# Token-major output projections: 512 columns at a time, the first half row by row of the weights for four blocks in four PSUM banks, the second half block by block

## The chip, the core and the metric

The kernel runs on one core of a Trainium2 chip. The metric is the device time of one execution in microseconds, 1507.78 us as the median of three runs (1503.12 to 1508.62). The work of the core is spread over TensorE (PE, with the weight loads shown apart as PEld), VectorE (DVE), ScalarE (ACT), GpSimd (POOL) and the queue on SyncE (SP) that issues nearly all DMAs. Every engine takes its instructions strictly in the order in which they stand; between engines they wait for each other by semaphores.

## The reference

Two token sequences (1024 and 512 tokens of width 1024, float32) go through two layers and a last RMSNorm. Cut to what matters here:

```
def attn_retention_layer(x, ...):           # layer 0: attention and retention
    z = rmsnorm(x, g) @ w_in ...
    mixed = concat([silu(ga) * oa, silu(gb) * ob], axis=-1)
    return x + mixed @ w_out                # first output projection
def windowed_layer(x, ...):                 # layer 1: windowed attention
    z = rmsnorm(x, g) @ w_in ...
    return x + (silu(gate) * o) @ w_out     # second output projection
y = rmsnorm(windowed_layer(attn_retention_layer(x)), final_norm)
```

`mixed` and `w_out` are both 1024 wide, so each output projection is a 1024 by 1024 matrix product for 1536 tokens.

## The kernel before

The 1536 tokens are 12 blocks of 128, in three groups `t` of four blocks (`GB`), which are handled in the order 2, 0, 1. A float32 product is made of three matmuls: both operands are split in a high part and the low remainder (`split`, L109; `load_w`, L130), and high by high, high by low and low by high are added in PSUM (`proj_tm_k`, L150). The gated branch of a group lies as `X["h", k, t]` and `X["l", k, t]`, eight rows `k` of 128 features by 512 tokens.

The output projections of groups 2 and 0 are feature-major (`out_proj_fm`, L266): their matmuls stream 512 tokens, and they are issued as filler between the pieces of the attention pipeline. At their end they need a sum over features: GpSimd adds squares into `acc` (L288), four small matmuls make `ssq`, then VectorE (`ms`), GpSimd (`rstd`) and VectorE (`dg`) make the factor, and four matmuls spread it as `R` (L293 to L299). For group 0 all this happens at the end of the pipeline.

The output projection of group 1 (`out_proj`, L324) is the one that changes. It is token-major: a block's 128 tokens are the stationary operand, the weights stream. It stands twice in the program, once for layer 0 (`woab`, the "first projection", some 793 to 850 us) and once for layer 1 (`woc`, the "second projection", some 1447 us to the end). Weights come in four chunks of 256 columns, each as four tiles of two rows `k`: a DMA into `wraw`, a copy to the high part on GpSimd (L139) and a subtraction for the low part on VectorE (L140). Tiles go alternately to the buffers `w` and `wg`, four each; `wg` is also the staging room of the feature-major projection. For each chunk the four blocks are taken one after the other; a block's 24 matmuls fill one of the three PSUM banks of `ps_any`, and VectorE adds the bank to the residual `xr` (L350). After the chunks comes `finish`: after layer 0 `norm_ab` (norm, scaling, transposes `trx`, and then the projection `pskv` of layer 1), after layer 1 `fin_c` (norm and output, L1092).

PSUM has eight banks here: five under the tag `s` (`ps_s` and `ps_t`, L57 to L61: scores, transposes `pte`, `ssq`, `R`) and three under `pj`. Tiles of a tag are handed out in the order of the program. A scheduler orders the instructions of each engine from priorities and from its own estimate of times; `tc.high_priority()` lifts a piece of code ahead.

Of the kernel before, what the change touches and what calls it, by code (L numbers as in the profile page):

```python
# [8 lines left out]
F32 = mybir.dt.float32  # L9
F32R = mybir.dt.float32r  # L10
AF = mybir.ActivationFunctionType
ALU = mybir.AluOpType
# [4 lines left out]
P = 128  # L17
# [5 lines left out]
GB = 4  # L23
CW = 256
# [12 lines left out]
def trunk_kernel(ctx, tc, x, xT, wab, woab, wc, woc, gT, qkg, ret, sink, relb, fng,  # L37
                 ropeA, ropeB, dist, kdist, qdist, onehot, wmask, out_p0, out_p1, out_s):
    nc = tc.nc
    dma = nc.sync.dma_start  # L40
# [3 lines left out]
    wp = ctx.enter_context(tc.tile_pool(name="wp", bufs=1))  # L44
# [8 lines left out]
    def buf(tag, name, n=None, dt=F32):  # L53
        t = wk.tile([P, SIZE[tag]], dt, tag=tag, name=name, bufs=BUFS[tag])
        return t if n is None else t[:, :n]

    def ps_s(name):  # L57
        return pp.tile([P, 512], F32, tag="s", name=name, bufs=5)
# [6 lines left out]
    def ps_p(name, use="fill"):  # L65
        free = ring[use]
        ring["i"] = next(i % 3 for i in range(ring["i"] + 1, ring["i"] + 4) if i % 3 in free)
        return pp.tile([P, 512], F32, tag=f"pj{ring['i']}", name=name, bufs=1)

    def ps_any(name):  # L70
        return ps_p(name, "all")
# [16 lines left out]
    def mm(ps, lhsT, rhs, start, stop):  # L88
        i = nc.tensor.matmul(ps, lhsT=lhsT, rhs=rhs, start=start, stop=stop)  # L89
        if pace["after"] is not None:  # L90
            tc.add_manual_dep(i.ins, pace["after"], order, reason="a filler keeps to its place in the pipeline")
            pace["after"] = None
        return i
# [36 lines left out]
    def load_w(arr, c, tag, lo=None, hook=None, ks=range(KT), raws=None):  # L130
        ts = {}
        for i in (k // 2 for k in ks[::2]):
            if raws is None:
                raw = wp.tile([P, 2 * CW], F32, tag="wraw", name="wraw", bufs=2)
                dma(out=raw, in_=arr[c, :, 2 * i:2 * i + 2, :].rearrange("p k n -> p (k n)"))
            else:
                raw = raws[i]
            w = wp.tile([P, 2, 2 * CW], F32R, tag=tag, name=tag, bufs=4)
            nc.gpsimd.tensor_scalar(w[:, 0, :], raw, 1.0, 1.0, ALU.mult, ALU.mult)  # L139
            (lo or nc.gpsimd).tensor_tensor(w[:, 1, :], raw, w[:, 0, :].bitcast(F32), ALU.subtract)  # L140
            ts[i] = w
            if hook is not None:
                hook(i)

        def get(s, k, a=0, n=CW):
            o = (k % 2) * CW + a
            return ts[k // 2][:, s, o:o + n]
        return get

    def proj_tm_k(ps, w, b, k, ks=range(KT)):  # L150
        t, o = b // GB, (b % GB) * P
        xh, xl = X["h", k, t][:, o:o + P], X["l", k, t][:, o:o + P]
        mm(ps, xh, w(0, k), k == ks[0], False)
        mm(ps, xh, w(1, k), False, False)
        mm(ps, xl, w(0, k), False, k == ks[-1])

    def proj_tm(ps, w, b, ks=range(KT)):
        for k in ks:
            proj_tm_k(ps, w, b, k, ks)

    def proj_pair(w, b, name):
        ps = ps_any(name)
        for j in range(2):
            proj_tm(ps[:, j * CW:(j + 1) * CW], w, b + j)
        return ps
# [28 lines left out]
    def load_block(src, name, tag="E"):  # L194
        hs = []
        for i in range(2):
            h = buf(tag, f"{name}{i}")
            dma(out=h, in_=src[:, i * 512:(i + 1) * 512])
            hs.append(h)
        return hs  # L200
# [121 lines left out]
                pass  # L322

    def out_proj(t, warr, ks, res, finish):  # L324
        def fetch(c):
            raws = {}
            for i in (k // 2 for k in ks[::2]):
                raws[i] = buf("E", "wraw")
                dma(out=raws[i], in_=warr[c, :, 2 * i:2 * i + 2, :].rearrange("p k n -> p (k n)"))
            return raws  # L330

        def convert(c, raws):
            return load_w(warr, c, "wg" if c % 2 else "w", nc.vector, None, ks, raws)

        with tc.high_priority():
            ws = [convert(0, None)]
        x1 = [load_block(res(t * GB + j), "xr") for j in range(GB)]
        raws = fetch(1)
        for c in range(4):
            w = ws[c]  # L340
            if c < 3:
                with tc.high_priority():
                    ws.append(convert(c + 1, raws))
                    raws = fetch(c + 2) if c < 2 else None
            for j in range(GB):
                ps = ps_any("pso")[:, :CW]
                proj_tm(ps, w, t * GB + j, ks)
                sl = x1[j][c // 2][:, (c % 2) * CW:(c % 2 + 1) * CW]
                with tc.high_priority():
                    nc.vector.tensor_tensor(sl, ps, sl, ALU.add)  # L350
        finish(t, x1)
# [43 lines left out]
    raws, xts = [], []  # L395
# [54 lines left out]
    for t in range(NG):  # L450
        pss = [(ps_any if t == 1 and j < 3 else ps_s)("pskv")[:, :CW] for j in range(GB)]
# [11 lines left out]
    ws = [load_w(wab, 0, "w")]  # L463
# [199 lines left out]
    for h in range(4):  # L663
        w = ws[h]
# [241 lines left out]

    x1_ab = []
    out_proj(1, woab, KS_A, lambda b: x[b], norm_ab)


    wkv = load_w(wc, 0, "w")
    kd_raw = {}
    for p in PAIRS:
        if p == PAIRS[4]:
            to_x(x1_ab, 1, 1)
        ps = proj_pair(wkv, 2 * p, "pskv").rearrange("p (b c) -> p b c", b=2)
# [175 lines left out]
    def fin_c(t, x2):  # L1092
        for j, hs in enumerate(x2):
# [4 lines left out]
            for i, h in enumerate(hs):  # L1098
                dma(out=out_p1[j][:, i * 512:(i + 1) * 512], in_=h)

    out_proj(1, woc, KS_C, lambda b: x1_d[b], fin_c)


# [90 lines left out]
```

## Time and profile before

| | us |
|---|---|
| median of three runs | 1507.78 |
| lowest and highest | 1503.12, 1508.62 |
| the profiled execution, its own time | 1507.83 |
| its span in the profile | 1506.1 |
| first projection, from the end of the work before it on TensorE to the first `pskv` | 793.1 to 850.4 |
| second projection, from the end of the feature-major matmuls to its last matmul | 1447.6 to 1496.4 |
| from that last matmul to the end of the span | 9.7 |

The span is what the engines' records cover; the execution's own time is 1.7 us longer. A row of the timeline gives the start, the duration from first to last of the merged instructions, the engine and line, the operation and, in brackets, how long the engine had been idle and who ended that. Matmuls overlap, so their pace is read from start to start.

### The profile page before, as it was taken

What the parts mean: (1) busy time and instruction counts of PE and PEld (TensorE: products, weight loads), DVE (VectorE), ACT (ScalarE), POOL (GpSimd) and SP (SyncE); (2) the same over time, 40 slices, a digit from 0 to 9 for tenths busy, and PEclk for the clock granted to TensorE, in tenths of its full rate; (3) what the DMA queues carried; (4) which work ended last, traced back from release to release, by engine and by line L of the source; (5) the groups of instructions that cost most, each with busy time, mean ns of one, the idle gap of its engine ahead of it and who ended that gap; (6) DMA issues with size and microseconds to landing.
All of it is one profiled execution on the core that took longest, in us unless ns stands there. A gap on an engine that the chain in (4) does not pass through costs nothing.

```text
span 1506.1 us, 26020 instructions
## 1 busy us (share of the span) xinstructions
PE 1451.7 (96%) x8734; PEld 1269.8 (84%) x8734; DVE 1052.6 (70%) x2431; ACT 719.5 (48%) x1770; POOL 812.3 (54%) x1044
## 2 busy tenths in 40 slices
PE   8999999989999999999999999999999999999997
PEld 8989999977888888777778998888888888777777
DVE  7455867686676666887978237687777767888774
ACT  5632222354555555555653245566556556645202
POOL 7654654474645484887887423342522532566542
PEclk9999999999999999999999999999999999999999
DMA  9631212326212143643664231121212211568752
GB/s 329 207 119 51 75 54 69 99 74 191 74 45 72 53 113 116 206 141 107 192 213 141 86 109 46 61 71 50 74 45 94 63 54 53 173 206 280 229 157 99
DMA packets 137333, 176.59 MB, mean 117 GB/s; under 512 B 38064, under 2 KB 66736, under 8 KB 137200
## 3 DMA queue, kind: packets, MB, share of 16 engines
q1 hardware_dynamic: 135040, 169.41, 35.8%
q0 software_dynamic: 2016, 5.51, 1.3%
q8 instruction: 69, 1.13, 0.3%
q14 instruction: 64, 0.52, 0.1%
q10 hardware_dynamic: 144, 0.01, 0.0%
HBM read 125.83 MB, written 53.25 MB: 119 GB/s over the span
## 4 chain that ended last, share of the span: by engine, by line
PE 71%; DVE 11%; DMA 4%; POOL 4%; issue 3%; ACT 1%; SPq 0%; POOLq 0%; DVEq 0%; ACTq 0%
PE psg L89 17%; PE psq L89 10%; PE po L89 8%; PE psb L89 8%; PE pso L89 8%; PE pte L173 7%; PE s L89 4%; PE sc L89 4%; PE pskv L89 2%; DVE xl L118 2%; DVE w L140 1%; DVE el L112 1%; DMA wraw<-in_woc 1%; DVE nm L837 1%; PE ptq L173 1%
## 5 line engine op out<-in xcount | busy, mean ns | idle before, releaser
L89 PE MATMUL psg<-xh,wg 128*128 128x512 f32 x768 | 263.9, 400 | 0.2 <-POOL wg L140 0.2
L107 POOL TENSOR_SCALAR ec<-ec,rl 128x384 f32<-128x384 f32 (+1 forms) x192 | 108.8, 581 | 241.5 <-DVE rl L1056 87.7
L112 DVE TENSOR_TENSOR el<-pte,eh 128x512 fp32r<-128x512 f32 x288 | 196.6, 685 | 56.2 <-ACT eh L111 32.5
L111 ACT ACTIVATE eh<-pte 128x512 fp32r<-128x512 f32 x288 | 170.1, 596 | 119.7 <-PE po L89 65.0
L89 PE MATMUL pso<-xh,w 128*128 128x512 f32 x512 | 183.6, 418 | 10.4 <-DVE w L140 4.6
L89 PEld LDWEIGHTS psg<-xh,wg 128*128 128x128 f32 x768 | 143.9, 189 | 29.2 <-POOL e L107 0.9
L107 POOL TENSOR_SCALAR e<-e,rl 128x512 f32<-128x512 f32 x160 | 114.3, 726 | 93.3 <-DVE rl L848 33.9
L89 PE MATMUL psg<-xl,wg 128*128 128x512 f32 x384 | 150.9, 393 | 0.0
L1051 ACT ACTIVATE ec<-ec,nm 128x384 f32<-128x384 f32 (+1 forms) x192 | 109.6, 572 | 82.7 <-DVE nm L1049 77.7
L845 ACT ACTIVATE e<-s,nm 128x512 f32<-128x512 f32 x160 | 108.9, 687 | 68.0 <-DVE nm L842 50.0
L837 DVE TENSOR_REDUCE nm<-s 128x1 f32<-128x512 f32 x160 | 107.8, 683 | 37.4 <-PE s L89 36.9
L139 POOL TENSOR_SCALAR w<-wraw 128x512 fp32r<-128x512 f32 x116 | 79.4, 686 | 97.6 <-PE pskv L89 32.4
L89 PE MATMUL psq<-xh,w 128*128 128x512 f32 x384 | 130.0, 397 | 0.0
L89 PEld LDWEIGHTS pso<-xh,w 128*128 128x128 f32 x512 | 99.4, 197 | 35.8 <-DVE w L140 7.8
L1045 DVE CUSTOM_DVE_ANT_0 ec<-sc,bias,sink_s 128x384 f32<-128x384 f32 (+1 forms) x192 | 105.3, 568 | 22.2 <-PE sc L89 17.8
L89 PE MATMUL pso<-xl,w 128*128 128x512 f32 x256 | 104.1, 408 | 2.0 <-DVE xl L118 2.0
L173 PE MATMUL pte<-ident,e 128*128 128x128 f32 x640 | 96.0, 275 | 1.6 <-POOL e L107 0.8
L173 PEld LDWEIGHTS pte<-ident,e 128*128 128x128 f32 x640 | 78.8, 142 | 20.3 <-ACT e L845 2.2
L140 POOL TENSOR_TENSOR w<-wraw,w 128x512 fp32r<-128x512 f32 x68 | 91.2, 1344 | 1.9
L89 PEld LDWEIGHTS psg<-xl,wg 128*128 128x128 f32 x384 | 72.5, 189 | 13.1
L89 PEld LDWEIGHTS psq<-xh,w 128*128 128x128 f32 x384 | 71.9, 188 | 13.6
L173 PE MATMUL pte<-ident,ec 128*128 128x128 f32 x512 | 79.0, 272 | 0.2
(230 smaller groups left out, 3942.6 us busy)
## 6 DMA issues: line engine op xcount, KB each, us to landing
wraw<-in_woab SPq DMA_DIRECT2D x48, 256.0 KB, 3.4
wraw<-in_woc SPq DMA_DIRECT2D x48, 256.0 KB, 3.8
wraw<-in_wab SPq DMA_DIRECT2D x44, 256.0 KB, 3.3
wraw<-in_wc SPq DMA_DIRECT2D x36, 256.0 KB, 3.1
xt<-in_xT SPq DMA_DIRECT2D x24, 256.0 KB, 5.4
xb<-in_x SPq DMA_DIRECT2D x24, 256.0 KB, 4.8
qd<-qd SPq DMA_DIRECT2D x48, 128.0 KB, 2.9
gab<-gz SPq DMA_DIRECT2D x24, 256.0 KB, 2.0
```

The costliest lines, as they stand in the source:

```text
L89: i = nc.tensor.matmul(ps, lhsT=lhsT, rhs=rhs, start=start, stop=stop)
L107: nc.gpsimd.tensor_scalar(o, i, s, 1.0, ALU.mult, ALU.mult)
L111: nc.scalar.activation(hi, src, AF.Copy)
L112: nc.vector.tensor_tensor(lo, src, hi.bitcast(F32), ALU.subtract)
L118: nc.vector.scalar_tensor_tensor(lo, src, scale, hi.bitcast(F32), ALU.mult, ALU.subtract)
L139: nc.gpsimd.tensor_scalar(w[:, 0, :], raw, 1.0, 1.0, ALU.mult, ALU.mult)
L140: (lo or nc.gpsimd).tensor_tensor(w[:, 1, :], raw, w[:, 0, :].bitcast(F32), ALU.subtract)
L173: return nc.tensor.transpose(o, i, ident)
L837: nc.vector.tensor_reduce(nm2[:, c:c + 1] if nh == 2 else nm[:, h:h + 1], s, AX.X, ALU.max, negate=True)
L845: nc.scalar.activation(eh[c], ss[c], AF.Exp, bias=nm[:, h:h + 1], accum_out=l[:, h, c:c + 1])
L1045: nc.vector.tensor_tensor_reduce(es[h][:, :nk], s, bias[h][:, bo:bo + nk], 1.0, sink_s[:, 4 * c + h:4 * c + h + 1], ALU.add, ALU.max, mx[: ...
L1051: nc.scalar.activation(es[a][:, :nk], es[a][:, :nk], AF.Exp, bias=nm[:, a:a + 1], accum_out=l[:, a:a + 1])
```

## The change

`out_proj` is rewritten. A weight tile is now one row `k` and 512 columns: two chunks of the same layout in the DRAM, so that a DMA's pieces are 256 columns long (1 KB) where they were 512 numbers (2 KB). Conversion is by the same two instructions. All eight tiles of the first 512 columns are fetched and converted with high priority; raw tiles use the two `wraw` buffers and buffers of the tag `E` in turn. The first half is done row by row: for each `k` the 12 matmuls of all four blocks, into four PSUM tiles of the tag `s`, and behind each row the tile of the same row of the second half is fetched. Then VectorE adds four banks of 512 columns. The second half is done block by block in banks of `ps_any`, the last block in two pieces of 256 columns. Numbers per projection: 384 matmuls of 256 columns before; now 168 of 512 columns and 48 of 256; 16 tiles as before, and 9 additions for 16.

```diff
     def out_proj(t, warr, ks, res, finish):
...
+        n = len(ks)
+
+        def fetch(i):
+            c, k = i // n, ks[i % n]
+            raw = wp.tile([P, 2 * CW], F32, tag="wraw", name="wraw", bufs=2) if i % 3 == 0 or i < 2 else buf("E", "wraw")
+            dma(out=raw.rearrange("p (c n) -> p c n", c=2), in_=warr[2 * c:2 * c + 2, :, k, :].rearrange("c p n -> p c n"))
+            w = wp.tile([P, 2, 2 * CW], F32R, tag="w" if i % n < 4 else "wg", name="wo", bufs=4)
+            nc.gpsimd.tensor_scalar(w[:, 0, :], raw, 1.0, 1.0, ALU.mult, ALU.mult)
+            nc.vector.tensor_tensor(w[:, 1, :], raw, w[:, 0, :].bitcast(F32), ALU.subtract)
+            ws[c, k] = w
+
+        ws = {}
         with tc.high_priority():
-            ws = [convert(0, None)]
+            for i in range(n):
+                fetch(i)
         x1 = [load_block(res(t * GB + j), "xr") for j in range(GB)]
-        raws = fetch(1)
-        for c in range(4):
-            w = ws[c]
-            if c < 3:
-                with tc.high_priority():
-                    ws.append(convert(c + 1, raws))
-                    raws = fetch(c + 2) if c < 2 else None
+        pss = [ps_s("pso") for j in range(GB)]
+        for i, k in enumerate(ks):
             for j in range(GB):
-                ps = ps_any("pso")[:, :CW]
-                proj_tm(ps, w, t * GB + j, ks)
-                sl = x1[j][c // 2][:, (c % 2) * CW:(c % 2 + 1) * CW]
+                proj_tm_k(pss[j], lambda s_, k_: ws[0, k_][:, s_, :], t * GB + j, k, ks)
+            with tc.high_priority():
+                fetch(n + i)
+        for j in range(GB):
+            with tc.high_priority():
+                nc.vector.tensor_tensor(x1[j][0], pss[j], x1[j][0], ALU.add)
+        for j in range(GB):
+            for a, m in ((0, 512),) if j < GB - 1 else ((0, CW), (CW, CW)):
+                ps = ps_any("pso")[:, :m]
+                proj_tm(ps, lambda s_, k_: ws[1, k_][:, s_, a:a + m], t * GB + j, ks)
+                sl = x1[j][1][:, a:a + m]
                 with tc.high_priority():
                     nc.vector.tensor_tensor(sl, ps, sl, ALU.add)
         finish(t, x1)
```

Where this moves instructions is seen in the order of the engines. First projection, TensorE, before: behind the transposes (`pte`) of the last attention unit some of its products (`po`) stand, and at once the new projection's matmuls (`pso<-w,xh`), with more `po` strewn among them further on.

```order
L173 MATMUL pte<-ident,e 128x128 x4
L89 MATMUL po<-eh,av 128x512
L89 MATMUL po<-el,av 128x512
L89 MATMUL po<-eh,av 128x512
L89 MATMUL po<-el,av 128x512
L89 MATMUL pso<-w,xh_9056 128x256 x2
L89 MATMUL pso<-w,xl_9057 128x256
L89 MATMUL pso<-w,xh_9198 128x256 x2
```

Now, the same place on TensorE from `ssq` on:

```order
L89 MATMUL ssq<-dg,acc 128x1 x4
L89 MATMUL po<-el,av 128x512
L89 MATMUL po<-eh,av 128x512
L89 MATMUL po<-el,av 128x512
L89 MATMUL po<-eh,av 128x512
L89 MATMUL po<-el,av 128x512
L89 MATMUL po<-eh,av 128x512
L89 MATMUL po<-el,av 128x512
L89 MATMUL R<-dg 128x128
L89 MATMUL pso<-wo,xh_9056 128x512 x2
L89 MATMUL pso<-wo,xl_9057 128x512
```

No matmul of the projection stands ahead of the last `po` and of the first `R` any more.

Second projection, TensorE, before, around `ssq`: the projection's matmuls stand on both sides of it, 56 of them between the last feature-major matmul and `ssq`.

```order
L89 MATMUL pso<-w,xl_16808 128x256
L89 MATMUL pso<-w,xh_16924 128x256 x2
L89 MATMUL pso<-w,xl_16925 128x256
L89 MATMUL pso<-w,xh_17018 128x256 x2
L89 MATMUL ssq<-dg,acc 128x1 x4
L89 MATMUL pso<-w,xl_17019 128x256
L89 MATMUL pso<-w,xh_17104 128x256 x2
```

Now, TensorE at the end of the feature-major matmuls (`pso<-xh,w`):

```order
L89 MATMUL pso<-xh_16521,w 128x512
L89 MATMUL pso<-xl_16522,w 128x512
L89 MATMUL pso<-xh_16521,w 128x512
L89 MATMUL ssq<-dg,acc 128x1 x4
L89 MATMUL R<-dg 128x128
L89 MATMUL pso<-wo,xh_16625 128x512 x2
L89 MATMUL pso<-wo,xl_16626 128x512
```

`ssq` and the first `R` follow the feature-major matmuls directly, and the projection starts behind them. On GpSimd the same place now reads as follows (`wo` are the new tiles' copies, `acc` the sums that `ssq` needs):

```order
L332 TENSOR_SCALAR wo<-wraw 128x512 x2
L288 TENSOR_TENSOR acc<-acc,sq 128x512
L332 TENSOR_SCALAR wo<-wraw 128x512 x2
L291 MEMSET dg 128x128
L332 TENSOR_SCALAR wo<-wraw 128x512
L288 TENSOR_TENSOR acc<-acc,sq 128x512
L332 TENSOR_SCALAR wo<-wraw 128x512 x2
L103 TENSOR_TENSOR rstd<-ms,nhalf 128x4
```

and on VectorE, where `ms` is the read of `ssq`:

```order
L283 TENSOR_TENSOR y<-pso,y 128x512
L333 TENSOR_TENSOR wo<-wraw,wo 128x512 x4
L100 TENSOR_SCALAR ms<-ssq 128x4
L333 TENSOR_TENSOR wo<-wraw,wo 128x512
L298 TENSOR_SCALAR dg<-ident,rstd 128x128 x4
```

Seven of the eight copies stand ahead of `rstd`, and four subtractions between the last `y` and `ms`.

End of the second projection, VectorE, before: the last bank's addition (L350) stands behind the output scaling (L1096) of the block before.

```order
L350 TENSOR_TENSOR xr_17598<-pso,xr_17598 128x256
L184 TENSOR_REDUCE ssum<-ss 128x1
L100 TENSOR_SCALAR ms<-ssum 128x1
L1096 SCALAR_TENSOR_TENSOR xr_17598<-xr_17598,rstd,fn 128x512
L350 TENSOR_TENSOR xr_17602<-pso,xr_17602 128x256
```

Now:

```order
L356 TENSOR_TENSOR xr_17436<-pso,xr_17436 128x512
L184 TENSOR_REDUCE ssum<-ss 128x1
L100 TENSOR_SCALAR ms<-ssum 128x1
L356 TENSOR_TENSOR xr_17440<-pso,xr_17440 128x256
L1102 SCALAR_TENSOR_TENSOR xr_17436<-xr_17436,rstd,fn 128x512
L356 TENSOR_TENSOR xr_17440<-pso,xr_17440 128x256
```

Two additions of the last block now follow the third block's, with the scaling between them; between the third block's last matmul and the last block's there are 48 matmuls where there were 24.

## Rows read from the trace of the kernel before

**Rows 1.** The page: shares of the span in the chain that ended last.

```profile
PE 71%; DVE 11%; DMA 4%; POOL 4%; issue 3%; ACT 1%; SPq 0%; POOLq 0%; DVEq 0%; ACTq 0%
```

**Rows 2.** Windows: stretch, length, busy per engine (instructions), PE clock, DMA share, GB/s.

```profile
793.10:850.40 57.30, 53.82 (x423) 51.63 (x422) 36.26 (x60) 17.68 (x42) 39.33 (x40) 1.00 0.44 137
1447.60:1496.40 48.80, 48.42 (x401) 47.90 (x399) 29.93 (x50) 7.45 (x23) 18.96 (x22) 1.00 0.36 115
```

**Rows 3.** Timeline of PE, second projection: start, duration, operation, [idle before <-releaser].

```profile
1445.30 0.62 PE L89 MATMUL pso<-xh,w 128*128 128x512 f32 x2
...
1447.36 0.39 PE L89 MATMUL pso<-xh,w 128*128 128x512 f32 x1
...
1454.84 1.05 PE L89 MATMUL ssq<-dg,acc 128*128 128x1 f32 x8 [0.38 <-POOL acc L288]
...
1459.92 1.06 PE L89 MATMUL R<-dg 128*128 128x128 f32 x8
...
1477.22 0.40 PE L89 MATMUL pso<-w,xh 128*128 128x256 f32 x2
...
1482.62 0.40 PE L89 MATMUL pso<-w,xh 128*128 128x256 f32 x2
...
1496.17 0.28 PE L89 MATMUL pso<-wg,xl 128*128 128x256 f32 x1
```

**Rows 4.** Timeline of PE, first projection.

```profile
805.58 1.17 PE L89 MATMUL R<-dg 128*128 128x128 f32 x8
...
820.19 0.50 PE L89 MATMUL pso<-wg,xh 128*128 128x256 f32 x2 [1.93 <-DVE xr L350]
```

**Rows 5.** Timeline of POOL, first projection, ahead of `R`.

```profile
802.88 0.62 POOL L139 TENSOR_SCALAR wg<-wraw 128x512 fp32r<-128x512 f32 x1 [5.49 <-DMA wraw<-in_woab]
```

**Rows 6.** Timelines of DVE, ACT and POOL, second projection, the steps ahead of `R`.

```profile
1445.74 1.77 DVE L140 TENSOR_TENSOR w<-wraw,w 128x512 fp32r<-128x512 f32 x1 [1.04 <-POOL w L139]
...
1449.25 0.68 DVE L140 TENSOR_TENSOR w<-wraw,w 128x512 fp32r<-128x512 f32 x1
1449.85 0.68 DVE L283 TENSOR_TENSOR y<-pso,y 128x512 f32<-128x512 f32 x1
...
1457.12 0.15 DVE L100 TENSOR_SCALAR ms<-ssq 128x4 f32<-128x4 f32 x1
1458.43 1.23 DVE L298 TENSOR_SCALAR dg<-ident,rstd 128x128 f32<-128x128 f32 x4 [1.15 <-POOL rstd L103]
...
1450.57 0.64 ACT L286 ACTIVATE sq<-y 128x512 f32<-128x512 f32 x1 [5.13 <-DVE y L283]
...
1445.67 1.29 POOL L288 TENSOR_TENSOR acc<-acc,sq 128x512 f32<-128x512 f32 x1
...
1453.07 1.72 POOL L288 TENSOR_TENSOR acc<-acc,sq 128x512 f32<-128x512 f32 x1
...
1457.36 1.03 POOL L103 TENSOR_TENSOR rstd<-ms,nhalf 128x4 f32<-128x4 f32 x1 [1.55 <-DVE ms L100]
```

**Rows 7.** Timeline of DVE, the end of the kernel.

```profile
1497.47 1.74 DVE L1096 SCALAR_TENSOR_TENSOR xr<-xr,rstd,fn 128x512 f32<-128x512 f32 x1 [0.67 <-POOL rstd L103]
1499.13 0.41 DVE L350 TENSOR_TENSOR xr<-pso,xr 128x256 f32<-128x256 f32 x1
...
1501.19 0.75 DVE L1096 SCALAR_TENSOR_TENSOR xr<-xr,rstd,fn 128x512 f32<-128x512 f32 x1 [0.67 <-POOL rstd L103]
```

**Rows 8.** Windows, a stretch of idle TensorE and the stretch behind it.

```profile
1437.90:1441.30 3.40, 1.64 (x6) 1.07 (x7) 2.26 (x2) 0.00 (x0) 2.83 (x3) 1.00 0.42 147
1441.30:1444.70 3.40, 3.40 (x10) 2.62 (x9) 3.40 (x4) 0.00 (x0) 1.67 (x2) 0.50 0.58 189
```

**Rows 9.** Timeline of POOL, the weights of `pskv` behind the first projection.

```profile
838.28 2.54 POOL L140 TENSOR_TENSOR w<-wraw,w 128x512 fp32r<-128x512 f32 x2
```

**Rows 10.** DMA issues by tile: count, KB each, median us to landing.

```profile
wraw<-in_woab SPq DMA_DIRECT2D x48, 256.0 KB, 3.4
zq<-qd SPq DMA_DIRECT2D x12, 128.0 KB, 2.5
```

More of the change, by code (lines that the diff above doesn't have):

```diff
@@ L324, in out_proj @@
     def out_proj(t, warr, ks, res, finish):
[L325 to L333, printed above, removed]
+        n = len(ks)
[7 more added lines that the diff above has]
+            ws[c, k] = w
```

## The prediction

> **What bounds the kernel now.** I read the chain of waits by engine first: TensorE carries 71% of it, VectorE 11%, GpSimd and DMA 4% each [rows 1]. So the two stretches that change are read from TensorE's side. The windows over them show it busy for 53.8 of 57.3 us in the first projection and for 48.4 of 48.8 in the second, at full granted clock, with the DMA engines under half busy [rows 2]. The reader is to see there that the second stretch has almost no hole to fill: a gain must come from shorter matmul time, and any new wait shows in full.
>
> Then the pace, from start to start in the timeline of TensorE. From 1477.22 to 1482.62 there are 45 matmuls of 256 columns in 5.40 us, 0.120 each; from 1445.30 to 1447.36 there are 9 of 512 columns in 2.06 us, 0.229 each [rows 3]. Two narrow ones take 0.240.
>
> Last, what ran while something else was slow. In both places the factor `R` of the feature-major projection has a long chain behind it. In the second, the feature-major matmuls end at about 1447.6 (1447.36 and one pace), `ssq` starts at 1454.84 and `R` at 1459.92 [rows 3], and the windows say that TensorE was busy nearly throughout: the narrow projection's matmuls filled these 12.3 us (56 of them, 6.7 us, stand ahead of `ssq`). In the first, `R` starts at 805.58 [rows 4], 12.5 us after the stretch begins at 793.1, with GpSimd idle 5.49 us before it, waiting for a raw weight tile [rows 5].
>
> **The change, part by part.**
>
> *Wider matmuls.* Before, 384 × 0.120 = 46.1 us per projection. After, 168 × 0.229 + 48 × 0.120 = 38.5 + 5.8 = 44.2; with the pace rounded up to 0.23, 44.4, which I use. It saves 1.7 per projection, all on the path.
>
> The timeline shows 0.229 for a wide matmul, at full clock [rows 3]. The Trainium skill, "TensorE: Matmul & The Clock Gate", section "Back-to-back issue gap", gives about 131 ns for 512 columns as the sustained figure of a stream of weight loads and matmuls. By it each projection would be some 168 × 0.098 = 16 us shorter, an estimate; the trace measures the very same shape in such a stream and disagrees, so I give it a chance of 0.01 and leave it out of the sum.
>
> *The order on TensorE.* The four PSUM tiles of the first half come from the tag that also serves scores, `ssq` and `R`, and are handed out behind them. By the order, no projection matmul stands ahead of the first `R` any more. What covered the chain to `R` is gone; the chain is now paid as idle time. This is the largest term, twice.
>
> First projection. Before, `R` came 12.5 us after 793.1; without GpSimd's wait for the raw tile it would be 7.0. The high-priority fetch may remove that wait, or not, since seven copies now stand before `rstd`. I take the middle, 9.7 (7.0 to 12.5). Within it lies the rest of attention's products.
>
> Second projection. After the last feature-major matmul come: `y` 0.68, `sq` 0.64, `acc` 1.29 to 1.72, `ssq` 1.05, `ms` 0.15, `rstd` 1.03, and the first of four `dg`, a quarter of 1.23, 0.31 [rows 3, 6]: 5.2 at the least. Four weight subtractions are queued on VectorE between `y` and `ms`. One took 0.68 alone and 1.77 beside GpSimd's `acc` [rows 6]: 2.7 to 7.1 together, beside `sq`, `acc` and `ssq`, which take 3.0 to 3.4. At their mean, 4.9, they overhang by 1.7. Two copies, 0.62 each [rows 5], stand on GpSimd between the last `acc` and `rstd`, beside 1.2 us of `ssq` and `ms`: about nothing if they aren't slowed. 5.2 + 1.7 is 6.9, and with the longer `acc` and half a microsecond of passing on, 7.6 (5.2 to 11.2; the upper end is the chain as long as before, when the first `dg` was done at 1458.43 + 0.31).
>
> In both, `R` itself then takes 0.8 until the projection starts (the row has 1.06 for all its small matmuls with the last one's overlapping end [rows 3]).
>
> *The clock.* The gap is followed by slow matmuls if the granted clock falls. In this trace a stretch of 3.40 us with TensorE busy for 1.64 was followed by one of 3.40 us at a granted clock of 0.50, that is 1.2 instead of 2.4 GHz [rows 8]. There matmuls take twice as long, so such a stretch costs half its length, 1.7. I take one spell at each projection (0 to 3.4, none or two).
>
> *Stalls that go.* At 820.19 TensorE waited 1.93 us for the addition that frees a bank [rows 4]. With four banks added only after the whole first half, and three others for the second, I expect none; the first stretch's other holes are of the same kind and are simply not in the new sum. Nothing in the second stretch had such a hole.
>
> *Weights of `pskv` behind the first projection.* Their tiles use the tag `w`, which is now read until the last piece of the last block: 24 × 0.12 = 2.9 us before the end the first of them come free. A tile costs GpSimd 0.62 [rows 5] and 1.27 [rows 9], 1.9. Before, this ran from 838 on, well ahead. If both of the first two are late, 3.8; I take a third, 1.3 (0 to 3.8). The transposes that now stand before `pskv` only change place.
>
> *The tail.* The stretch from the last matmul to the end took 9.7 us. The last addition started at 1499.13, behind a scaling of 1.74 us that started at 1497.47, though its bank was complete at about 1496.4: 2.7 us late [rows 3, 7]. Now there are 48 matmuls between the third block's end and the last, 5.8 us instead of 2.9, so that scaling should be past. I take 7.0 (7.0 to 9.7).
>
> *Edits at nothing.* DMA pieces of 1 KB instead of 2 KB: a tile took 3.4 us to land; `zq`, 128 KB in 1 KB pieces, took 2.5 [rows 10], so 256 KB take 3.4 to 5.0. Hidden by the fetch ahead of the first eight; uncovered it costs what the rival of the late weight rows costs. Supply: TensorE spends 12 × 0.23 = 2.76 us on a row of the weights; converting one costs GpSimd 0.62 and VectorE 0.68 [rows 5, 6]. Nine wide additions for 16 narrow ones: VectorE was busy 30 of 48.8 us [rows 2], so this is cover.
>
> **Sum.** First projection: 9.7 + 0.8 + 44.4 + 1.7 + 1.3 = 57.9 for 57.3, that is +0.6; all terms low 7.0 + 0.8 + 44.4 = 52.2 (−5.1), all high 12.5 + 0.8 + 44.4 + 3.4 + 3.8 = 64.9 (+7.6). Second with its tail: 7.6 + 0.8 + 44.4 + 1.7 + 7.0 = 61.5 for 48.8 + 9.7 = 58.5, +3.0; low 57.4 (−1.1), high 69.5 (+11.0). Together +3.6. On the profiled execution's own time of 1507.83, which is the median of the runs but for 0.05, that is 1511.4, rounded 1511. In words: the wide matmuls and the better tail give back about 6 us, the uncovered chains and the clock take about 10.
>
> **The rivals.**
>
> *The gaps stay short.* GpSimd's wait goes wholly, the subtractions hide, the clock holds, `pskv` is not delayed: −6.2, 1502. For it: a chain that has no narrow additions in its way on VectorE any more. Against: it needs everything low at once. About half of such cases pass −7.5.
>
> *The chains grow (slower).* GpSimd and VectorE slow each other while eight tiles are converted at high priority, just where `ssq`, `rstd` and `dg` queue behind them; the gaps are then as long as before, 12.5 and 11.2 (+6.4 on my sum), with two clock spells in each (+3.4): 1511.4 + 9.8 = 1521. For it: the subtraction's 1.77 beside `acc` against 0.68 alone [rows 6]. It decides from an `R` about 2 us later than I take it in each place. The Trainium skill, "SBUF — State Buffer", section "Who interferes with whom", says that a VectorE instruction with two SBUF inputs contends with a GpSimd instruction that reads SBUF; the two durations agree with it, and by it the conversion at high priority would be the worst neighbour for that chain.
>
> *Weight rows late.* The row-by-row half wants a converted row every 2.76 us. In the second projection two subtractions stood 3.5 us apart (1445.74 and 1449.25) [rows 6]. If that became the pace, 8 × 0.74 = 5.9 per projection, 1523. Against: the first eight are fetched well ahead, and 0.62 + 0.68 is half of 2.76. It decides as soon as a row takes longer than 2.76.
>
> *It doesn't do what it says*: the reordering leaves the narrow projection's filler in place. The order shows no such thing; under 0.02.
>
> **How the numbers follow.** Forecast 0.50, near 1511 (its own range 1506 to 1517). Short gaps 0.17; long chains 0.15; late rows 0.10; the remaining 0.08 are mixtures on either side. A measurement of this kernel tells a change from none at about 0.5%, 7.5 us: faster than 1500.2, slower than 1515.3. Faster: half of the short gaps and some of the rest, 0.11. Slower: both long cases and a twentieth from the upper end of the forecast, 0.29. Same 0.60. The range that leaves out 2 in 10 is 1500 to 1521.
>
> **What would show it.** Right: in the second projection, TensorE idle for 6 to 9 us between its last feature-major matmul and `R`, `ssq` following `acc` at once, one stretch at granted clock 0.50 behind it; 512-column `pso` at 0.23 from start to start; no wait inside the first half; the last addition at once behind its bank; a tail near 7. Wrong: an `R` within 5 us or beyond 11; waits for `wo` between rows of the first half; TensorE idle for more than 2 us before `pskv`; or a wide pace clearly under 0.22, which would make everything 10 us or more shorter.

## The result and the profile after

The changed kernel takes 1516.82 us (median of 7 runs, 1514.2 to 1519.6), the kernel before 1508.62 (7 runs, 1503.12 to 1510.67). The ratio is 1.0059 with a 95% interval of 1.0046 to 1.0071: 8.2 us slower, and within 6.9 to 10.7. The forecast was 1511, +3.6. Its way was right and its size less than half.

Its profiled execution has a span of 1516.7 us, 10.6 more than before. Three landmarks tell where they are: the first matmul of `psq`, which follows the first projection and `pskv`, the last feature-major matmul, and the end.

| kernel, one profiled execution each | first `psq` at | `psq` to last feature-major | from there to the end | span |
|---|---|---|---|---|
| before | 890.5 | 556.8 | 58.7 | 1506.1 |
| changed | 896.9 | 556.3 | 63.5 | 1516.7 |

(A landmark is the start of the first or the last matmul named.) So 6.4 us were lost at the first projection and its `pskv`, 4.8 at the second with its tail, and 0.5 came back between. The two profiled executions lie 1.7 us above and 0.8 us below their medians, hence 10.6 here and 8.2 above.

**The second gap** answers to [rows 3]. TensorE in the changed kernel: start, duration, operation, and in brackets the idle time and who ended it.

```profile
1453.19 0.39 PE L89 MATMUL pso<-xh,w 128*128 128x512 f32 x1
1459.00 1.87 PE L89 MATMUL ssq<-dg,acc 128*128 128x1 f32 x8 [5.42 <-POOL acc L288]
1463.04 0.80 PE L89 MATMUL R<-dg 128*128 128x128 f32 x2 [2.17 <-DVE dg L298]
1463.49 1.20 PE L89 MATMUL pso<-wo,xh 128*128 128x512 f32 x2
...
1509.67 0.28 PE L89 MATMUL pso<-wo,xl 128*128 128x256 f32 x1
```

Between the last feature-major matmul and `R` TensorE does nothing but `ssq`. `R` comes 9.6 us behind 1453.42; forecast 7.6, at most 11.2. The windows of the same stretch (columns as in [rows 2]) show the clock:

```profile
1453.40:1456.80 3.40, 0.17 (x1) 0.00 (x0) 2.35 (x4) 0.14 (x1) 3.06 (x5) 0.99 0.35 117
1456.80:1460.20 3.40, 1.20 (x6) 1.20 (x6) 2.89 (x4) 0.49 (x1) 2.83 (x3) 0.50 0.68 233
1460.20:1463.60 3.40, 1.23 (x7) 1.14 (x6) 2.45 (x7) 0.00 (x0) 1.77 (x2) 0.50 0.58 183
1463.60:1467.00 3.40, 3.40 (x10) 2.67 (x9) 0.00 (x0) 0.00 (x0) 0.00 (x0) 0.50 0.15 52
```

The granted clock is 0.50 (1.2 of 2.4 GHz) already inside the gap and for one stretch behind it, where 3.40 us of matmul time do the work of 1.70. VectorE in the gap, to be read against [rows 6]:

```profile
1452.45 1.77 DVE L333 TENSOR_TENSOR wo<-wraw,wo 128x512 fp32r<-128x512 f32 x1 [1.31 <-POOL wo L332]
1455.27 0.75 DVE L1072 SCALAR_TENSOR_TENSOR yn<-yn,g_sb,rb 128x512 f32<-128x512 f32 x1 [1.05 <-DMA yn<-x2T]
1455.94 0.69 DVE L283 TENSOR_TENSOR y<-pso,y 128x512 f32<-128x512 f32 x1
1456.54 2.95 DVE L333 TENSOR_TENSOR wo<-wraw,wo 128x512 fp32r<-128x512 f32 x3
1460.00 1.09 DVE L333 TENSOR_TENSOR wo<-wraw,wo 128x512 fp32r<-128x512 f32 x1 [0.51 <-POOL wo L332]
1461.01 0.15 DVE L100 TENSOR_SCALAR ms<-ssq 128x4 f32<-128x4 f32 x1
```

The last `y` starts 2.5 us after its bank is complete, because a subtraction and a product `yn` that waits for its DMA stand ahead of it; then four subtractions stand ahead of `ms`. From the start of `y` to `R` it takes 7.1 us, here and in the three later runs that leave this chain as it is (e3, e6, e7). The start of `y` itself varies: 1.5 (e7), 2.6 (e3) and 3.7 us (e6) behind its bank, 2.5 here. So the gap's length differs between traces by up to 2 us (8.5 to 10.8) with no edit to it.

**The first gap** answers to [rows 4]. TensorE:

```profile
796.80 0.50 PE L89 MATMUL po<-eh,av 128*128 128x512 f32 x1 [2.50 <-ACT eh L111]
799.20 0.79 PE L89 MATMUL po<-el,av 128*128 128x512 f32 x1 [1.90 <-DVE el L112]
...
801.93 1.70 PE L89 MATMUL ssq<-dg,acc 128*128 128x1 f32 x8
...
806.69 0.63 PE L89 MATMUL R<-dg 128*128 128x128 f32 x2
806.97 1.20 PE L89 MATMUL pso<-wo,xh 128*128 128x512 f32 x2
```

and its windows:

```profile
793.10:796.50 3.40, 1.16 (x4) 0.67 (x4) 3.40 (x6) 1.49 (x4) 3.11 (x4) 1.00 0.34 116
796.50:799.90 3.40, 1.20 (x3) 0.79 (x4) 3.40 (x6) 1.96 (x4) 2.47 (x3) 0.72 0.77 251
799.90:803.30 3.40, 3.40 (x16) 3.00 (x14) 2.78 (x4) 1.19 (x2) 1.50 (x2) 0.50 0.81 254
803.30:806.70 3.40, 3.40 (x10) 2.43 (x11) 2.65 (x8) 0.60 (x1) 1.02 (x1) 0.50 0.92 305
```

Attention's last products wait for their split operands while VectorE is full: 2.50 us for `eh`, which ScalarE makes, and 1.90 for `el`, which VectorE makes. ScalarE before `eh`:

```profile
794.35 0.51 ACT L117 ACTIVATE xh<-oT 128x128 fp32r<-128x128 f32 x2 [3.32 <-POOL oT L725]
795.50 0.63 ACT L286 ACTIVATE y<-y 128x512 f32<-128x512 f32 x1 [0.64 <-DVE y L283]
796.15 0.60 ACT L111 ACTIVATE eh<-pte 128x512 fp32r<-128x512 f32 x1
```

So `eh` stood in the queue behind `xh`, which waited for GpSimd, and behind a square of `y`, which waited for VectorE. Then the clock is at half, and the rest of attention, `ssq` and `R` run at 1.2 GHz (a `po` every 0.43 us). `R` comes 13.6 us behind 793.1: forecast 9.7, at most 12.5.

**Behind the first projection** TensorE waits for `pskv`'s weights, once, and GpSimd before that for raw tiles:

```profile
862.21 0.39 PE L89 MATMUL pskv<-w,xh 128*128 128x256 f32 x1 [2.17 <-POOL w L140]
```

```profile
851.59 1.20 POOL L139 TENSOR_SCALAR w<-wraw 128x512 fp32r<-128x512 f32 x2
852.76 2.52 POOL L140 TENSOR_TENSOR w<-wraw,w 128x512 fp32r<-128x512 f32 x2
858.67 0.62 POOL L139 TENSOR_SCALAR w<-wraw 128x512 fp32r<-128x512 f32 x1 [1.42 <-DMA wraw<-in_wc]
860.31 0.62 POOL L139 TENSOR_SCALAR w<-wraw 128x512 fp32r<-128x512 f32 x1 [1.02 <-DMA wraw<-in_wc]
860.89 2.51 POOL L140 TENSOR_TENSOR w<-wraw,w 128x512 fp32r<-128x512 f32 x2
```

The first two tiles are converted from 851.59 on, where it was 836.98 before, and TensorE does not wait for them: transposes `trx` and `pskv` fill the time. The wait falls on the third. There are two raw buffers, and they came free only with the first two subtractions (852.76 to 855.28); the chain that ended last shows the fetch behind the second of them (start, duration, what):

```profile
855.30 4.85 DMA wraw<-in_wc
```

GpSimd's queue has the fourth tile's copy, which waited for this fetch, ahead of the third tile's subtraction, which `pskv` needs.

**The tail** answers to [rows 7]. VectorE at the end:

```profile
1507.45 1.31 DVE L1102 SCALAR_TENSOR_TENSOR xr<-xr,rstd,fn 128x512 f32<-128x512 f32 x1
1509.99 0.42 DVE L356 TENSOR_TENSOR xr<-pso,xr 128x256 f32<-128x256 f32 x1 [1.23 <-PE pso L89]
```

The last addition starts as soon as its bank is complete; from the last matmul's end, 1509.95, to the end of the span are 6.8 us.

### The profile page after: what moved, and what is told of

The parts are those of the page before. It is cut to its first block, busy times and chain, and to the rows that moved or that the text cites. A ratio compares the mean times of both kernels' runs of the same rounds, so it can differ in the third digit from the quotient of the medians.

```text
span 1516.7 us, 25326 instructions
## 1 busy us (share of the span) xinstructions
PE 1454.9 (96%) x8398; PEld 1257.4 (83%) x8398; DVE 1052.4 (69%) x2417; ACT 718.7 (47%) x1770; POOL 808.6 (53%) x1044
## 4 chain that ended last, share of the span: by engine, by line
PE 68%; DVE 10%; DMA 6%; POOL 4%; issue 4%; ACT 1%; SPq 0%; POOLq 0%; DVEq 0%; ACTq 0%
PE psg L89 17%; PE psq L89 10%; PE psb L89 8%; PE po L89 8%; PE pso L89 6%; PE pte L173 6%; PE s L89 4%; PE sc L89 3%; PE pskv L89 2%; DVE xl L118 2%; DVE el L112 1%; DMA wraw<-in_woc 1%; DMA yn<-x2T 1%; DVE w L140 1%; DVE nm L843 1%
## 5 line engine op out<-in xcount | busy, mean ns | idle before, releaser
L139 POOL TENSOR_SCALAR w<-wraw 128x512 fp32r<-128x512 f32 x100 | 66.6, 667 | 77.2 <-PE pskv L89 29.7
L89 PE MATMUL pso<-wo,xh 128*128 128x512 f32 (+1 forms) x288 | 83.3, 374 | 0.2
```

## The experiments

Theory A: the loss is filler that went. The four tiles `pso` of tag `s` are handed out behind `ssq` and `R`, so nothing covers these chains. Theory B: the weight conversions at high priority lengthen the chains, and the order of TensorE is secondary. Each kernel was timed in rounds with the kernel before (1508.0 to 1508.8 in the three groups).

**e1: the banks exchanged.** First half in the three `pj` banks and one of tag `s`, second half in tag `s`:

```diff
-        pss = [ps_s("pso") for j in range(GB)]
+        pss = [ps_any("pso") if j < 3 else ps_s("pso") for j in range(GB)]
...
-                ps = ps_any("pso")[:, :m]
+                ps = ps_s("pso")[:, :m]
```

> The change with the PSUM banks exchanged: first half in the three pj banks and one of tag s, second half in tag s; in the order the projection's matmuls stand again ahead of ssq and R at both places. Theory A (the loss is the filler that went, since four banks of tag s are handed out behind ssq and R): TensorE busy through both gaps, granted clock 1.00 there; the wide matmuls (-1.7 each), the better tail (-2.7) and the vanished bank stalls come out, only the late pskv weights stay: about 1503, faster than before by 3 to 7 us. Theory B (the conversions of the weights at high priority slow the chain to R and attention's end): these are the same here, so R stays as late, 1514 or more.

Measured: 1500.13, ratio 0.9943 [0.9929, 0.9956], 7.8 us faster than before. TensorE around the second `R`, and the windows of that stretch:

```profile
1444.88 0.39 PE L89 MATMUL pso<-xh,w 128*128 128x512 f32 x1
1445.10 0.62 PE L89 MATMUL pso<-wo,xh 128*128 128x512 f32 x2
...
1459.43 1.05 PE L89 MATMUL R<-dg 128*128 128x128 f32 x8
```

```profile
1444.80:1448.20 3.40, 3.40 (x17) 2.67 (x15) 2.75 (x3) 0.00 (x0) 3.38 (x5) 1.00 0.50 171
...
1451.60:1455.00 3.40, 3.40 (x21) 2.94 (x20) 1.76 (x3) 0.00 (x0) 1.90 (x3) 1.00 0.43 142
```

`R` comes 14.3 us behind the feature-major matmuls, later than in the changed kernel, and it costs nothing: the projection's matmuls fill the time at full clock. Theory A holds. Theory B's conversions are all still there. From the last feature-major matmul to the end it takes 53.4 us, 5.3 less than before; the first `psq` comes at 888.3, 2.2 earlier. A new wait appeared inside the first projection:

```profile
822.21 0.74 PE L89 MATMUL pso<-wo,xh 128*128 128x512 f32 x2 [2.32 <-ACT xh L117]
```

Another of 0.75 us for `xl` followed at 823.70. Here the last attention block's product with its gate stood behind seven products `yn` on GpSimd.

**e2 and e3: the change at one projection only**, the other calling the old function:

```diff
-    out_proj(1, woc, KS_C, lambda b: x1_d[b], fin_c)
+    out_proj_old(1, woc, KS_C, lambda b: x1_d[b], fin_c)
```

(e2; in e3 the call with `woab` is the one that goes to `out_proj_old`.)

> The change at the first projection alone, the second as before. From the two traces (the landmarks of layer 1 stand 6.4 to 6.7 us later from the first psq on): 1515, +6.5 on the kernel before, of which some 3 us behind the projection, at the weights of pskv. Rival: the first place costs nothing by itself and the shift comes from elsewhere: 1508.

> The change at the second projection alone. From the two traces (from the last feature-major matmul to the end 63.3 us instead of 58.5): 1513, +4.8 on the kernel before: gap to R 9.6, one spell of half clock in the projection, tail 7.0. Rival: without the change at the first place the weights' traffic meets the gap otherwise and the gap is short, near 5: 1509.

Measured: e2 1511.58, 1.0024 [1.0014, 1.0035], +3.6; e3 1513.99, 1.0036 [1.0023, 1.0048], +6.0. Together 9.6, the whole change 8.2. The landmarks: first `psq` at 896.1 in e2 and at 890.5 in e3; from the last feature-major matmul to the end 59.5 in e2 and 63.9 in e3. Each place loses by itself. By the medians the first loses less than expected and the second more. In e2's trace 5.6 us are lost ahead of `psq` and 2.7 made up in layer 1 (554.1 us to the last feature-major matmul instead of 556.8). Why was not tried; that stretch has the same code in every run and took 552.6 to 556.8 us in their traces, so a difference of this size needs no cause in the change.

**e4: no subtractions.** The low parts of the new weight tiles are left out; ScalarE copies the raw tile in their place.

```diff
-            nc.vector.tensor_tensor(w[:, 1, :], raw, w[:, 0, :].bitcast(F32), ALU.subtract)
+            nc.scalar.activation(w[:, 1, :], raw, AF.Copy)
```

> The low parts of the new weight tiles are left out: ScalarE copies the raw tile in their place, so VectorE has no subtraction of these tiles. Theory A: the chain gets shorter by the subtractions that stand between y and ms (some 2 us in the second gap) and attention's el comes earlier (some 2 to 3 us in the first), but TensorE still idles: 4 to 7 us in each gap, total 1512. Theory B (VectorE's share of the conversions is the cause): both gaps nearly vanish (R within 5 us of the last feature-major matmul, no wait over 1 us for el), total 1507 or less.

Measured: 1512.31, 1.0025 [1.0014, 1.0035], 4.5 less than the changed kernel. Its profiled execution, 1505.36, was the shortest of eleven and 7 us below their median, so the trace is no typical one. TensorE at both places:

```profile
791.64 0.67 PE L89 MATMUL po<-eh,av 128*128 128x512 f32 x1 [2.18 <-ACT eh L111]
...
1441.78 0.39 PE L89 MATMUL pso<-xh,w 128*128 128x512 f32 x1
1446.64 1.40 PE L89 MATMUL ssq<-dg,acc 128*128 128x1 f32 x8 [4.47 <-POOL acc L288]
1449.73 0.79 PE L89 MATMUL R<-dg 128*128 128x128 f32 x2 [1.69 <-DVE dg L298]
```

The gap to `R` is 7.7 us instead of 9.6, the first one (from the last feature-major matmul) 10.7 instead of 14.2. At the second place `y` to `R` takes 5.8 us instead of 7.1, so 1.3 us are the subtractions' there; the other 0.6 is the start of `y`, which varies by more. At the first, other traces of the same code have 12.6 to 14.8 us, so 10.7 lies outside their spread. There the wait for `el` went from 1.90 to 0.23 us, but the one for `eh` stayed, 2.18 for 2.50: now ScalarE's copies stood ahead of it, so e4 can't tell what of that wait is due to the subtractions. By the times, leaving them out gives back 4.5 of the 8.2 us. But most of each gap stays, and e1 has all of them and loses nothing: theory B is a part, and A the ground.

**e5 and e9: unused matmuls in the second gap.** 24 of 512 columns ahead of `ssq` (e5); 32 ahead and 14 behind (e9, whose edit is shown, without the helper `junk` that issues them):

```diff
+        junk(32)
         ps = ps_s("ssq")
         for j in range(GB):
-            mm(ps[:, j:j + 1], acc[:, j * P:(j + 1) * P], one[:, 0:1], True, True)
+            q = mm(ps[:, j:j + 1], acc[:, j * P:(j + 1) * P], one[:, 0:1], True, True)
+        junk(14, q.ins.name)
```

> The changed kernel with 24 further matmuls of 512 columns, whose result nobody reads, between the last feature-major matmul and ssq of the second projection: it fills TensorE's idle time and leaves every wait as it is. If the gap is paid twice, as idle time and as half clock behind it: granted clock 1.00 from ssq on, R still 8 to 9.5 us behind the last feature-major matmul (ssq and R themselves faster by about 1), the first projection matmuls at 0.23 instead of 0.43, 2 to 3 us less: 1514. If the clock has another cause than the idle TensorE: half clock stays, 1517.

> As e5, with 32 unused matmuls ahead of ssq and 14 behind it, so that TensorE stays busy until about R. If the half clock behind the gap follows from the idle TensorE: granted clock 1.00 throughout, the projection's first matmuls at 0.23, about 1.7 us less than e5 behind R. If it doesn't: half clock for about 3.4 us again behind R.

Measured: e5 1514.63, 1.0045 [1.0031, 1.0058]; e9 1514.92, 1.0042 [1.0028, 1.0055]. Neither is clear of the changed kernel's interval, so the traces must decide. In e5 `y` came late, 4.5 us behind its bank, the fill ended 2.3 us ahead of `ssq`, the granted clock fell to 0.50 again and the first matmuls behind `R` were slow: its expectation failed at the clock, and it tells only that this fill was too short. In e9 the fill reached `R`:

```profile
1451.47 7.42 PE L89 MATMUL junk<-xh,xh 128*128 128x512 f32 x32
1458.73 0.95 PE L89 MATMUL ssq<-dg,acc 128*128 128x1 f32 x8
1459.54 3.47 PE L89 MATMUL junk<-xh,xh 128*128 128x512 f32 x14
1462.84 0.38 PE L89 MATMUL R<-dg 128*128 128x128 f32 x2
1462.98 0.71 PE L89 MATMUL pso<-wo,xh 128*128 128x512 f32 x2
```

```profile
1459.20:1462.60 3.40, 3.40 (x18) 2.86 (x18) 2.18 (x7) 0.00 (x0) 1.12 (x2) 1.00 0.64 195
1462.60:1466.00 3.40, 3.40 (x19) 2.86 (x18) 0.00 (x0) 0.00 (x0) 0.00 (x0) 1.00 0.11 39
```

The clock stays at 1.00, and the projection takes 44.85 us (1462.98 to 1507.83) instead of 46.46 (1463.49 to 1509.95): 1.6 less, the clock's term. `ssq` took 0.95 instead of 1.87 us. The fill itself held `ssq` back by about 1.1 us (`acc` was done at 1457.67), and `y` started 3.2 us behind its bank instead of 2.5; the gap to `R` was 11.4 us instead of 9.6, which is why so little shows in the total.

**e6: `pskv`'s weights earlier**, raw tiles fetched ahead of the output writes and low parts on VectorE:

```diff
     def norm_ab(t, x1):
+        with tc.high_priority():
+            for i in range(KT // 2):
+                wkv_raws[i] = buf("E", "wraw")
+                dma(out=wkv_raws[i], in_=wc[0, :, 2 * i:2 * i + 2, :].rearrange("p k n -> p (k n)"))
...
-    wkv = load_w(wc, 0, "w")
+    wkv = load_w(wc, 0, "w", nc.vector, None, range(KT), wkv_raws)
```

> The changed kernel with the raw weights of pskv fetched ahead of the first projection's output writes, and their low parts made on VectorE instead of GpSimd. If the 3.8 us more between the last matmul of the first projection and the first psq come from late weights (the wait of 2.17 us for a tile of w and the half clock behind it): no wait over 0.5 us there, 3 to 4 us less: 1513. If the transposes that moved ahead of pskv are it: nothing, 1517.

Measured: 1512.80, 1.0035 [1.0024, 1.0046], 4.0 less than the changed kernel, whose interval it just touches. Window of TensorE where the wait of 2.17 us was:

```profile
856.00:862.00 6.00, 6.00 (x53) 6.00 (x52) 0.37 (x2) 1.34 (x5) 0.00 (x0) 1.00 0.00 0
```

From the projection's end to the first `psq` it takes 41.5 us, 43.7 in the changed kernel, 40.0 before. The late weights were worth 2.2 of the 3.7 us; the rest is not assigned (a new wait of 1.05 us at 876.35 for transposed input is in it). The edit does two things at once, earlier raw tiles in buffers of their own and subtractions on VectorE, and the run can't tell them apart. It leaves the tag `w` as it is: GpSimd's four copies stand between 848.49 and 851.73 without a wait.

**e7: the wide matmuls of the projections cut in two.**

```diff
+                for a in (0, CW):
...
+                    p, wh, wl = pss[j][:, a:a + CW], ws[0, k][:, 0, a:a + CW], ws[0, k][:, 1, a:a + CW]
...
-            for a, m in ((0, 512),) if j < GB - 1 else ((0, CW), (CW, CW)):
+            for a, m in ((0, CW), (CW, CW)):
```

> The changed kernel with every wide matmul of the projections cut in two of 256 columns, all else in its place. If the pace of the matmuls counts: 168 x (0.240 - 0.229) = 1.8 us more per projection, 1520.5. If the supply of weight rows or the gaps set the time: no difference, 1517.

Measured: 1520.25, 1.0078 [1.0064, 1.0091], +3.4 on the changed kernel against 3.6 expected. The intervals of the two overlap a little (1.0064 and 1.0071), so the size is supported and not proved by the times. The second projection takes 49.4 us instead of 46.5, and the first 47.5 instead of 46.2.

**e8 and e11: what the exchanged banks left.** `yn` behind the gate product and, the last four, behind pairs of weight copies (e8, cut to the main lines); the last six behind such pairs, and e6's early weights (e11):

```diff
-        nc.gpsimd.tensor_tensor(y, y, rb, ALU.mult)
+        i = nc.gpsimd.tensor_tensor(y, y, rb, ALU.mult)
+        if t == 0:
+            tc.add_manual_dep(i.ins, lastof["mix"], order, reason="behind the last block's product")
+            if k >= 4:
+                tc.add_manual_dep(i.ins, lastof["copy"][(k - 4) * 2 + 1], order, reason="behind two copies of weights")
```

> The kernel with exchanged banks, and GpSimd's eight products yn at the first projection put behind the last attention block's product with its gate and, the last four, behind pairs of copies of the second half's weights. The waits of 2.32 and 0.75 us near 822 and the half clock behind them go: 3 to 5 us less than the 1500.1 of exchanged banks, 1496. Rival: yn comes too late for pskv or the copies stay the bound, and the wait only moves: 1500.

> Exchanged banks, with GpSimd's products yn behind the last attention block's product and, from the third on, behind pairs of copies of the second half's weights, and with the weights of pskv fetched early and their low parts made on VectorE. If e8 stood still because the copies came late and pskv waited for GpSimd (1.4 us of waits for wo near 832 and 1.4 for w near 853): these go, 1497. If another wait takes their place: 1500.

Measured: e8 1499.92, 0.9941 [0.9928, 0.9954]; e11 1500.62, 0.9951 [0.9933, 0.9969]. Both are e1 again, and both expectations fell to their rivals. The waits near 822 went, and others came, in e8:

```profile
830.66 0.50 PE L89 MATMUL pso<-wo,xh 128*128 128x512 f32 x1 [0.73 <-DVE wo L338]
```

and in e11 one of 1.94 us for `wo` at 835.84 (its profiled execution, 1506.58, was the longest of six). e11 aimed at e8's waits for `wo` and `w`, about 1.4 us each: those for `w` went, those for `wo` grew to 2.7. That GpSimd and VectorE have the same work in this stretch, whichever goes first, would explain it and is not shown.

**e10: the last `y` ahead of `yn`** (cut to the main lines).

```diff
+        if ylast:
+            tc.add_manual_dep(i.ins, ylast[0], order, reason="behind the last y")
```

> The changed kernel with the last y of the second projection's feature-major part put ahead of the product yn (L1072) that stood before it on VectorE and waited 1.05 us for its DMA. If the gap was longer than forecast because y stood 2.5 us late in VectorE's queue: y within 1 us of the last feature-major matmul, gap to R 7.5 to 8.5 instead of 9.6, total 1515. If the subtractions of the weights ahead of ms set it: the gap stays above 9.

Measured: 1515.26, 1.0042 [1.0029, 1.0055], not clear of the changed kernel. VectorE:

```profile
1450.72 0.68 DVE L286 TENSOR_TENSOR y<-pso,y 128x512 f32<-128x512 f32 x1
...
1452.33 4.79 DVE L340 TENSOR_TENSOR wo<-wraw,wo 128x512 fp32r<-128x512 f32 x4
1457.05 0.15 DVE L100 TENSOR_SCALAR ms<-ssq 128x4 f32<-128x4 f32 x1
```

`y` came 1.0 us behind the matmuls instead of 2.5, yet `R` 9.3 us instead of 9.6. The theory that `y`'s place alone was what the forecast lacked falls: `yn` and then the four subtractions, which take 4.79 us, now stand between `y` and `ms`, and from `y` to `R` it takes 8.3 us instead of 7.1.

## Why the prediction was right, and where it was too small

- *The order on TensorE*, the largest term: right, and shown by e1, e2 and e3. With the filler back, the same wide matmuls make the kernel faster than before.
- *First gap, 9.7 (7.0 to 12.5)*: mis-sized, 13.6 measured. This is the term that failed most. I took the chain to `R` of before and shortened it. I did not see that with an empty TensorE attention's own drain becomes the path: its products waited 4.4 us for split operands, and the clock fell inside the gap, so that the rest of the chain ran at half speed. That the subtractions are behind the wait for `el` (1.90 us) is shown by e4; how much of the wait for `eh` (2.50) is theirs stays open.
- *Second gap, 7.6 (5.2 to 11.2)*: inside the bounds, 2.0 too small. The overhang of the subtractions was right in kind: they took 1.20 us each in e10, and I had taken 1.23. The chain from `y` on took 7.1 us, near the sum, and that although `ssq` runs at half clock, which the sum did not have. What the sum put at nothing is that `y` itself starts 2.5 us behind its bank. e10 shows that moving `y` alone doesn't give this back.
- *The clock behind the gap, 1.7 each*: right at the second place (1.6 by e9). At the first, the loss fell largely inside the gap: from 799.90 to 806.70 the granted clock is 0.50, in the 3.40 us behind 806.70 it is 0.78.
- *Wide matmuls, 1.7 saved per projection*: right. In the changed kernel 15 of them stand between 1499.96 and 1503.36, 0.227 each, and with the clock kept up the projection took 44.85 (e9) against 44.4 in the sum. e7 gives 3.4 for both projections and the last blocks.
- *`pskv`'s weights, 1.3 (0 to 3.8)*: too small, and the mechanism right only at its start. The tiles of the tag `w` are converted late, as forecast, but the first two, which the sum priced, cost nothing; what cost 2.17 us of waiting was the fetch of the next raw tiles behind them, which the sum did not have. `psq` came 3.7 us later behind the projection; e6 takes 2.2 of them away in the trace and 4.0 us off the median, and one of the signs named for "wrong", more than 2 us of idle TensorE at `pskv`, was met, though inside `pskv` and not before it.
- *Stalls that go and the tail, 7.0*: right. There is no wait for a bank from `R` to the end of the first projection, and the tail is 6.8; in e2, with the old second projection, it is 9.4.

The sum, redone with what the traces show: first projection 3.9 more for the gap, 0.5 less for `R`, 2.4 more for `pskv`, so +6.4 instead of +0.6; second 2.0 more for the gap, the rest within 0.4 a term, so +4.8 instead of +3.0. The excess is therefore in the two gaps and at `pskv`, and hardly any of it in the matmuls or the tail. That the total stayed inside the stated range owes something to its width: the first gap alone lay outside its own bounds.

The rivals: the long chains came about half way true in the second place, in the first fully. Weight rows late did not: between 810 and 853 TensorE had no wait for `wo`.

The Trainium skill, "SBUF — State Buffer", section "Who interferes with whom", was named for VectorE's two-input subtractions beside GpSimd. The traces agree: 0.68 us alone, 1.20 on the mean of four beside GpSimd's copies and `acc` in e10, up to 1.77. "TensorE: Matmul & The Clock Gate", section "Back-to-back issue gap", gives 131 ns for 512 columns; 0.227 us measured here decides against it for this kernel's operands.

## What to carry to other kernels

Where a new piece of work is to begin beside the tail of another, look from which pool its first PSUM tile comes and what is handed out from it just before: here that decided whether the matmuls could serve as filler, and was worth 16 us between two versions that differ in two lines. A gap on TensorE cost its length here and something more behind it, since the granted clock fell inside it: `ssq`, which is in the chain that it waits for, took twice as long, and so did the first matmuls after it. When a cover goes, sum the chain from every engine's queue as it will then stand, not from the old trace's intervals.

## What the hardware showed that was not expected

The half clock set in during the waiting, not only behind it: `ssq` took 1.87 us in the changed kernel's gap against 0.95 in e9, whose only difference there is that TensorE was kept busy with unused matmuls. The chain that ends a gap can so be lengthened by the gap. And two rearrangements of GpSimd's work at the first projection, on top of the exchanged banks, did not move the time: 1500.13 without (e1), 1499.92 and 1500.62 with them (e8, e11), though the waits near 822 went. What binds that stretch then stays open.
